# Banded attention of a two-layer decoder: two heads at a time, their scores alternating between the halves of the array's rows

## Chip, core and metric

The kernel runs on one core of a Trainium2 chip. The metric is the device time of one launch in microseconds. The core's engines work side by side, each through its own queue in order: TensorE (PE in the profile; its weight loads are shown apart as PEld), VectorE (DVE), ScalarE (ACT), GpSimd (POOL, hardly used here) and the DMA queue that SyncE (SP) issues.

## The reference

Two layers of a decoder trunk on 256 tokens with 2048 features. Each layer has a mixer (four mLSTM heads beside 16 heads of sliding-window attention) and an MLP of 8192 hidden features. The part that the change touches, cut down:

```python
# q (B,S,16,64); k, v (B,S,4,64): four query heads share one head of keys
# queries in blocks of T = 128; each block sees its own block of keys and the one before
scores = einsum('bnqhgd,bnkhd->bnhgqk', qb, kb)            # sums over 64 features
scores = where(valid, scores - slope_h * dist, -inf)       # 0 <= dist < 128
m = maximum(max(scores), sink_h)
p = exp(scores - m)
probs = p / (sum(p) + exp(sink_h - m))
out = einsum('bnhgqk,bnkhd->bnqhgd', probs, vb)
ha = rms_norm(out.reshape(B, S, 1024), g_attn_out)
```

The attention's result stands beside the mLSTM's, goes through the out-projection, a norm and the MLP.

## The kernel before

**Weights.** All weight matrices are streamed once from DRAM in loads of 1 MiB (tile `raw`, six buffers). Two k-tiles by 512 columns make a slab. ScalarE copies a slab to a rounded high part (`whi`, L232) and VectorE subtracts it for the low part (`wlo`, L236); four buffers of each. TensorE multiplies three products per k-tile (high by high, high by low, low by high), all at L329: 24 matmuls of 256 columns per slab where the weights are stationary (`qa`, `qm`, `km`, `up`), 12 of 512 columns where the tokens are (`vm`, `om`, `op`, `dn`). The loads of w_ada pass through the same `raw` buffers and are summed on VectorE (L204).

**Work beside the stream.** Everything else in a mixer is a set of Python generators (`Task`). Ahead of each slab's matmuls every task advances by one stage (`side`), so its instructions stand in the engines' queues between those of two slabs; after that a scheduler may shift them a little in the queues. PSUM tiles for this work come from a pool of four (`ps_x`, counted by `live["x"]`), tiles of 128x384 from a pool of seven (`live["w"]`).

**Attention** (`swa`, `swa_head`, `swa_out`). The query projection is laid out so that a tile `qa` of a unit u holds eight heads: heads 8u to 8u+3 on partitions 0 to 63, heads 8u+4 to 8u+7 on partitions 64 to 127; the keys `kaT` likewise. `swa` starts one head per slab, up to four in flight, in the order 0, 1, 2, ... 15. A head's stages are one slab apart:

1. Scores: two matmuls over 64 partitions into one PSUM tile `pss` (L591: 128 queries by 128 keys; L592: 128 queries by 256 keys). Each float32 matmul shows in the trace as two loads and two passes.
2. VectorE adds the distances times the slope (tile `s`, L595), takes the maxima (L598, L599) and the bias `nm` (L600).
3. ScalarE takes the exponentials and their sums (L602, L603).
4. Three transposes on TensorE into `pt` (L609).
5. ScalarE copies them to `sT` (L612).
6. Three matmuls with the values into `po` (L618 to L620), which collects four heads.

After four heads, `swa_out` normalises their 256 columns (L627 to L637) and sums squares (L84), and only then may the next group of four start. After the fourth group a norm over the 1024 features follows (L677 to L682), and the flag `swa` lets the mLSTM's outputs (`pn`, L852 to L854) begin. Their norms and gates (`rm`, `frs`, `va`) and the transposes `psct` (L909) lead to the out-projection `op`.

Of the kernel before, what the change touches and what calls it, by code (L numbers as in the profile page):

```python
# [27 lines left out]
# column offsets in the packed small parameters  # L28
# [5 lines left out]
# shape-only constants: identity | banded distances | causal bias  # L34
# [5 lines left out]
def hymba_kernel(ctx: ExitStack, tc: tile.TileContext, x_d, c_d, cols_d, cons_d, wada_d,  # L40
# [70 lines left out]
    # ("w", blocks of (unit, first k-tile), source) of weights; ("a", layer, vector, pair of feature tiles) of w_ada  # L111
# [9 lines left out]
    def weave(ws, *segments):  # L121
        """ws, with the entries ads of each segment (ads, start, upto) spread evenly over that range of ws."""
# [41 lines left out]
    # each entry in two loads  # L164
# [33 lines left out]
    def ada_op():  # L198
        """Sums over the input features for one tile of 128 output features."""
# [87 lines left out]
    class Unit:  # L287
        """Products with one block of 512 weight columns, accumulated in two PSUM banks."""
# [22 lines left out]
        def slabs_by_token(self, between):  # L311
            """Four slabs, all for the first token tile and then all for the second."""
# [42 lines left out]
    # gate rows (times the post-norm gain) broadcast over the partitions  # L355
# [17 lines left out]
    class PreNorm:  # L373
        """Residual update (with yg), RMSNorm, modulation and transposition of x."""
# [34 lines left out]
        def group(self, g, tok):  # L409
            """Transposed activations of four k-tiles, in two parts."""  # L410
# [18 lines left out]
        def turn_in(self, xnT, tok, g0=0):  # L429
            """Transposition of one token tile from k-tile 4 g0 on, before the modulation is known."""  # L430
# [12 lines left out]
        def modulate(self, e, xnT, hfp):  # L443
            """Two k-tiles of the activations."""
# [79 lines left out]
    for l in range(DEPTH):  # L524
# [59 lines left out]
        def swa_head(h, po):  # L584
            u, hh = h // 8, h % 8
            base, j = 64 * (hh // 4), hh % 4
            qt = fl["qa", u][base:base + 64, j, :]
            kt_ = kaT[base:base + 64, u, :]
            live["w"] += 1
            pss = xalloc(f"pss{L}_{h}")  # L590
            T.matmul(pss[:, 0:P], qt[:, TK[0]], kt_[:, TK[0]], start=True, stop=True)  # L591
            T.matmul(pss[:, P:3 * P], qt[:, TK[1]], kt_, start=True, stop=True)  # L592
            yield
            s = walloc(f"s{L}_{h}", 0)
            V.scalar_tensor_tensor(s, dist, -(2.0 ** (-8.0 * (h + 1) / 16.0)), pss[:, 0:384],  # L595
                                   ALU.mult, ALU.add)
            xdone()
            V.tensor_reduce(mx[:, h, 0:1], s[:, 0:P], AX.X, ALU.max)  # L598
            V.tensor_reduce(mx[:, h, 1:2], s[:, P:384], AX.X, ALU.max)  # L599
            V.tensor_scalar(nm[:, h, :], mx[:, h, :], sk[:, h:h + 1], -1.0, ALU.max, ALU.mult)  # L600
            yield
            A.activation(s[:, 0:P], s[:, 0:P], AF.Exp, bias=nm[:, h, 0:1], accum_out=sm[:, h, 0:1])  # L602
            A.activation(s[:, P:384], s[:, P:384], AF.Exp, bias=nm[:, h, 1:2], accum_out=sm[:, h, 1:2])  # L603
            yield
            while live["x"] > 3:
                yield
            pt = xalloc(f"pt{L}_{h}")
            for b in range(3):
                T.transpose(pt[:, b * P:(b + 1) * P], s[:, b * P:(b + 1) * P], ident)  # L609
            yield  # L610
            sT = walloc(f"sT{L}_{h}", 0)
            A.activation(sT, pt[:, 0:384], AF.Copy)  # L612
            xdone()
            yield
            vs = slice((h // 4) * 64, (h // 4) * 64 + 64)
            c0 = (h % 4) * 64
            o0, o1 = po[:, c0:c0 + 64], po[:, 256 + c0:256 + c0 + 64]
            T.matmul(o0, sT[:, 0:P], vat[:, 0, vs], start=True, stop=True)  # L618
            T.matmul(o1, sT[:, P:2 * P], vat[:, 0, vs], start=True, stop=False)
            T.matmul(o1, sT[:, 2 * P:3 * P], vat[:, 1, vs], start=False, stop=True)  # L620
            live["w"] -= 1

        def swa_out(g, po):
            """Normalisation of four heads and their sums of squares."""
            hs = slice(4 * g, 4 * g + 4)
            for b in range(2):
                V.tensor_tensor(es[:, hs, b], nm[:, hs, b], sk[:, hs], ALU.add)  # L627
            A.activation(es[:, hs, :], es[:, hs, :], AF.Exp)
            V.tensor_tensor(sm[:, hs, :], sm[:, hs, :], es[:, hs, :], ALU.add)
            V.reciprocal(sm[:, hs, :], sm[:, hs, :])  # L630
            yield
            o0 = (g % 2) * 256
            for b in range(2):
                if g % 2 == 0:
                    ha[g // 2, b] = ytile(f"ha{L}_{g // 2}_{b}")
                o = ha[g // 2, b][:, o0:o0 + 256]
                V.tensor_tensor(o.rearrange("p (h d) -> p h d", h=4),  # L637
                                po[:, b * 256:b * 256 + 256].rearrange("p (h d) -> p h d", h=4),
                                sm[:, hs, b:b + 1].broadcast_to([P, 4, 64]), ALU.mult)
            xdone()  # L640
            yield
            for b in range(2):
                square_sum(ha[g // 2, b][:, o0:o0 + 256], ssa[:, b, g:g + 1], f"jka{L}_{g}_{b}")
            yield

        def swa():
            while ("qa", 0) not in fl or "kv" not in fl:
                yield
            fly, nxt, outs, po = [], 0, [], None
            while nxt < 16 or fly or outs:  # L650
                for f in list(fly):
                    try:
# [3 lines left out]
                        live["q"] -= f[1] % 8 == 7  # L656
                        if f[1] % 4 == 3:
                            outs.append(swa_out(f[1] // 4, f[2]))
                            po = None
# [5 lines left out]
                ok = nxt < 16 and len(fly) < 4 and ("qa", nxt // 8) in fl  # L665
                if ok and nxt % 4 == 0:
                    ok = po is None and live["x"] <= 1
                    if ok:
                        po = xalloc(f"po{L}_{nxt // 4}")
                if ok and live["x"] <= 3 and live["w"] <= 6 and po is not None:  # L670
                    f = (swa_head(nxt, po), nxt, po)
# [48 lines left out]
        def gates():  # L720
# [29 lines left out]
            # log sigmoid(f) = min(f, 0) - log1p(exp(-|f|)), log1p(t) = log(w) + (t - (w - 1)) / w with w = 1 + t  # L750
# [16 lines left out]
            # u = i - b, g = running maximum of u (from the stabiliser before the chunk), m = b + g  # L767
# [10 lines left out]
            # columns: u (two chunks), u + B (first chunk), exp(-m) (two chunks)  # L778
# [25 lines left out]
        def mlstm_weights(h):  # L804
            """exp(u_s - g_t) times q k, [source position, target position]."""
# [215 lines left out]
        def evac_up_tokens(un, u):  # L1021
            """As evac_up, for products with tokens on the partitions."""
# [181 lines left out]
```

## Time and profile before

| | us |
|---|---|
| median of three timed runs | 2284.05 (2282.85 to 2285.39) |
| span of the profiled execution | 2283.6 |
| TensorE busy | 2195.6 |
| VectorE busy | 1690.7 |
| ScalarE busy | 1090.9 |
| start of layer 0's first score matmul | 160.8 |
| start of layer 1's first score matmul | 1256.0 |

The profile gives no time of its own for the profiled execution beside its span, from the first to the last instruction; the timed runs have no profile. In the views that follow, a row names line, engine, operation and tiles as out<-in, then counts and times. "64*128" on a matmul is the part of the array it uses, rows by columns. A merged timeline row "x2" covers two instructions from the first start to the last end. A matmul's shown length includes its way through the array; how fast a row of them goes is read from start to start.

### The profile page before, as it was taken

The page shows a single profiled execution, that of the slowest core. Times are in us where ns is not written, and L with a number is a line of the kernel's source. Part 1 is how long each engine was busy: PE and PEld are TensorE (multiplying, and loading weights), DVE is VectorE, ACT ScalarE, POOL GpSimd, SP SyncE. Part 2 cuts the span into 40 slices and gives each one's busy share as a digit, 9 for nine tenths or more (in the row PEclk, how much of TensorE's full clock was granted, in tenths as well). Part 3 has the DMA queues.
Part 4 walks back from the last instruction along what each step waited for, and adds up shares of the span by engine and source line. Part 5 has one row for each costly group of instructions (what it writes and reads, how often), then busy time and mean ns, then how long its engine had stood idle before and what let it go on. Part 6 is the DMA issues. An engine that isn't in the chain of part 4 may idle for free.

```text
span 2283.6 us, 33092 instructions
## 1 busy us (share of the span) xinstructions
PE 2195.6 (96%) x13322; PEld 1935.3 (85%) x13322; DVE 1690.7 (74%) x2282; ACT 1090.9 (48%) x1533; POOL 1.4 (0%) x14
## 2 busy tenths in 40 slices
PE   6789999899999999999989999989999999999998
PEld 5679777698898998989869988878898998998986
DVE  7988899787878877877577797957556656555556
ACT  4346663645444444434464566556443444444433
POOL 0000000000000000000000000000000000000000
PEclk9999999999999999999999999999999999999999
DMA  9997679497888888888538766845656666555551
GB/s 370 385 360 273 221 300 365 171 356 307 315 299 336 308 309 312 316 305 300 185 128 336 294 223 215 294 165 197 234 213 230 229 223 248 203 185 186 184 187 70
DMA packets 82363, 590.08 MB, mean 258 GB/s; under 512 B 9185, under 2 KB 9633, under 8 KB 10785
## 3 DMA queue, kind: packets, MB, share of 16 engines
q1 hardware_dynamic: 82210, 587.98, 69.4%
q8 instruction: 104, 1.70, 0.3%
q14 instruction: 49, 0.40, 0.0%
HBM read 585.81 MB, written 2.13 MB: 257 GB/s over the span
## 4 chain that ended last, share of the span: by engine, by line
PE 77%; DVE 4%; ACT 1%; issue 1%; DVEq 0%; ACTq 0%
PE up L329 32%; PE dn L329 31%; PE op L329 4%; PE qa L329 2%; PE vm L329 2%; PE om L329 1%; PE km L329 1%; PE qm L329 1%; PE kva L329 1%; DVE x L388 1%; DVE wlo L236 1%; PE pss L592 0%; PE pss L591 0%; ACT jkm L84 0%; PE psgate L730 0%
## 5 line engine op out<-in xcount | busy, mean ns | idle before, releaser
L236 DVE TENSOR_TENSOR wlo<-raw,whi 128x1024 fp32r<-128x1024 f32 x720 | 876.6, 1222 | 472.2 <-ACT whi L232 470.9
L232 ACT ACTIVATE whi<-raw 128x1024 fp32r<-128x1024 f32 x720 | 758.5, 1058 | 915.3 <-PE dn L329 376.0
L329 PE MATMUL up<-hthm,whi 128*128 128x256 f32 x1920 | 543.7, 283 | 0.0
L329 PE MATMUL up<-hthm,wlo 128*128 128x256 f32 x1920 | 543.3, 283 | 0.0
L329 PE MATMUL up<-htlm,whi 128*128 128x256 f32 x1920 | 543.2, 283 | 0.0
L204 DVE SCALAR_TENSOR_TENSOR raw<-raw,cact 128x2048 f32<-128x2048 f32 x192 | 437.3, 2285 | 4.1 <-DMA raw<-in_wada_dram 4.0
L329 PE MATMUL dn<-whi,sh 128*128 128x512 f32 x1024 | 404.1, 395 | 0.0
L329 PE MATMUL dn<-wlo,sh 128*128 128x512 f32 x1024 | 404.0, 395 | 0.0
L329 PE MATMUL dn<-whi,sl 128*128 128x512 f32 x1024 | 404.0, 395 | 0.0
L329 PEld LDWEIGHTS up<-htlm,whi 128*128 128x128 f32 x1920 | 368.4, 192 | 0.9
L329 PEld LDWEIGHTS up<-hthm,whi 128*128 128x128 f32 x1920 | 368.4, 192 | 0.9
L329 PEld LDWEIGHTS up<-hthm,wlo 128*128 128x128 f32 x1920 | 368.4, 192 | 0.0
L329 PEld LDWEIGHTS dn<-wlo,sh 128*128 128x128 f32 x1024 | 192.9, 188 | 45.0
L329 PEld LDWEIGHTS dn<-whi,sh 128*128 128x128 f32 x1024 | 193.0, 188 | 44.7 <-ACT sh L1034 0.4
L329 PEld LDWEIGHTS dn<-whi,sl 128*128 128x128 f32 x1024 | 192.9, 188 | 44.4 <-DVE sl L1035 0.2
L329 PE MATMUL op<-wlo,cth 128*128 128x512 f32 x256 | 99.6, 395 | 2.8 <-DVE wlo L236 2.8
L329 PE MATMUL op<-whi,cth 128*128 128x512 f32 x256 | 99.2, 396 | 2.6 <-ACT whi L232 2.6
L329 PE MATMUL op<-whi,ctl 128*128 128x512 f32 x256 | 100.2, 393 | 0.0
L329 PE MATMUL vm<-whi,htha 128*128 128x512 f32 x128 | 57.0, 447 | 28.7 <-ACT whi L232 18.7
L1064 DVE TENSOR_TENSOR ys<-ys,dn 128x512 f32<-128x512 f32 x112 | 75.4, 685 | 5.2 <-PE dn L329 4.6
L329 PE MATMUL qa<-htha,whi 128*128 128x256 f32 x256 | 73.2, 286 | 0.0
L329 PE MATMUL qa<-htla,whi 128*128 128x256 f32 x256 | 72.4, 283 | 0.0
(275 smaller groups left out, 2545.1 us busy)
## 6 DMA issues: line engine op xcount, KB each, us to landing
raw<-in_wada_dram SPq DMA_DIRECT2D x192, 1024.0 KB, 6.4
raw<-in_wdn_dram SPq DMA_DIRECT2D x128, 1024.0 KB, 5.0
raw<-in_wup_dram SPq DMA_DIRECT2D x120, 1024.0 KB, 4.9
raw<-in_win_dram SPq DMA_DIRECT2D x56, 1024.0 KB, 5.0
raw<-in_wout_dram SPq DMA_DIRECT2D x32, 1024.0 KB, 6.8
raw<-in_wst_dram SPq DMA_DIRECT2D x16, 1024.0 KB, 6.6
raw<-in_wsu_dram SPq DMA_DIRECT2D x8, 1024.0 KB, 6.2
gp<-gdr SPq DMA_DIRECT2D x4, 1024.0 KB, 4.7
```

What stands on the lines that cost most here:

```text
L204: V.scalar_tensor_tensor(w, w, 1.0, cact, ALU.mult, ALU.mult, accum_out=modc[l][:, v, j:j + 1])
L232: A.activation(hi, raw, AF.Copy)
L236: V.tensor_tensor(lo, raw, hi.bitcast(F32), ALU.subtract)
L329: T.matmul(o, a, w, start=not self.started[b], stop=last and i == 2, skip_group_check=True)
L388: V.scalar_tensor_tensor(xc, self.yg[c][tok], r, xc, ALU.mult, ALU.add)
L1064: V.tensor_tensor(yt, yt, ps[tok], ALU.add)
```

## The change

Two heads that share a `qa` tile's column but lie on its two halves (h and h + 4) form a pair. Their scores go into two PSUM tiles, and the four matmuls alternate: lower half, upper half, lower half, upper half. Vector and scalar stages run for both heads one after the other; transposes, copies and value matmuls for the first head of the pair, then, two slabs later, for the second. Pairs are started in the order (0,4), (1,5), (2,6), (3,7), (8,12), (9,13), (10,14), (11,15), one per slab, up to three in flight; a group that shares a `po` tile is now two pairs, for instance heads 0, 4, 1, 5. `swa_out` reads and writes its four heads with a stride. Nothing is computed differently. Comments are removed as well, which shifts the line numbers.

```diff
-        def swa_head(h, po):
-            u, hh = h // 8, h % 8
-            base, j = 64 * (hh // 4), hh % 4
-            qt = fl["qa", u][base:base + 64, j, :]
-            kt_ = kaT[base:base + 64, u, :]
-            live["w"] += 1
-            pss = xalloc(f"pss{L}_{h}")
-            T.matmul(pss[:, 0:P], qt[:, TK[0]], kt_[:, TK[0]], start=True, stop=True)
-            T.matmul(pss[:, P:3 * P], qt[:, TK[1]], kt_, start=True, stop=True)
-            yield
-            s = walloc(f"s{L}_{h}", 0)
-            V.scalar_tensor_tensor(s, dist, -(2.0 ** (-8.0 * (h + 1) / 16.0)), pss[:, 0:384],
-                                   ALU.mult, ALU.add)
...
+        def swa_pair(h, po):
+            u, j, heads = h // 8, h % 4, (h, h + 4)
+            live["w"] += 2
+            pss = [xalloc(f"pss{L}_{g}") for g in heads]
+            for c0, c1, tok, keys in ((0, P, 0, TK[0]), (P, 3 * P, 1, slice(0, S))):
+                for a in range(2):
+                    rows = slice(64 * a, 64 * a + 64)
+                    T.matmul(pss[a][:, c0:c1], fl["qa", u][rows, j, TK[tok]], kaT[rows, u, keys],
+                             start=True, stop=True)
+            yield
+            s = [walloc(f"s{L}_{g}", 0) for g in heads]
+            for a, g in enumerate(heads):
+                V.scalar_tensor_tensor(s[a], dist, -(2.0 ** (-8.0 * (g + 1) / 16.0)), pss[a][:, 0:384],
+                                       ALU.mult, ALU.add)
+                xdone()
+                V.tensor_reduce(mx[:, g, 0:1], s[a][:, 0:P], AX.X, ALU.max)
+                V.tensor_reduce(mx[:, g, 1:2], s[a][:, P:384], AX.X, ALU.max)
+                V.tensor_scalar(nm[:, g, :], mx[:, g, :], sk[:, g:g + 1], -1.0, ALU.max, ALU.mult)
+            yield
...
+            for a, g in enumerate(heads):
+                while live["x"] > 3:
+                    yield
+                pt = xalloc(f"pt{L}_{g}")
+                for b in range(3):
+                    T.transpose(pt[:, b * P:(b + 1) * P], s[a][:, b * P:(b + 1) * P], ident)
+                yield
+                sT = walloc(f"sT{L}_{g}", 0)
+                A.activation(sT, pt[:, 0:384], AF.Copy)
+                xdone()
+                yield
...
+            pairs = [8 * u + 2 * i + b for u in range(2) for i in range(2) for b in range(2)]
...
-                ok = nxt < 16 and len(fly) < 4 and ("qa", nxt // 8) in fl
-                if ok and nxt % 4 == 0:
+                ok = nxt < 8 and len(fly) < 3 and ("qa", nxt // 4) in fl
+                if ok and nxt % 2 == 0:
...
-                if ok and live["x"] <= 3 and live["w"] <= 6 and po is not None:
-                    f = (swa_head(nxt, po), nxt, po)
+                if ok and live["x"] <= 2 and live["w"] <= 5 and po is not None:
+                    f = (swa_pair(pairs[nxt], po), nxt, po)
```

What this does to the queues is shown at three places. First, TensorE's queue in layer 1 where the attention starts, between two slabs of `qa` (the number behind `pss_` is the head):

```order
 L329 MATMUL qa_1_11270<-htla_0_10420,whi_11211 128x256
 L329 MATMUL qa_1_11270<-htha_0_10419,wlo_11212 128x256
-L591 MATMUL pss_0_11309<-kaT_10809,qa_0_11277 128x128
-L592 MATMUL pss_0_11309<-kaT_10809,qa_0_11277 128x256
+L596 MATMUL pss_0_11309<-kaT_10809,qa_0_11277 128x128
+L596 MATMUL pss_4_11310<-kaT_10809,qa_0_11277 128x128
+L596 MATMUL pss_0_11309<-kaT_10809,qa_0_11277 128x256
+L596 MATMUL pss_4_11310<-kaT_10809,qa_0_11277 128x256
 L329 MATMUL qa_0_11269<-htha_0_10419,whi_11240 128x256
 L329 MATMUL qa_0_11269<-htla_0_10420,whi_11240 128x256
```

Heads 0 and 4 now stand between these two slabs, alternating; behind the next slab follow heads 1 and 5, and behind the six slabs after that no scores at all. The first transposes stand three slabs behind the scores, as before. All eight pairs of layer 1 look like this.

Second, TensorE's queue in layer 0, in the slabs of `om` (the scheduler's order; `pscol` are small transposes of the mLSTM's gates, 4 rows high, `pg` a matmul of theirs):

```order
L596 MATMUL pss_11_2424<-kaT_1291,qa_1_1315 128x128
L799 MATMUL pscol_2365<-cons,rows_2088 128x4 x2
L596 MATMUL pss_11_2424<-kaT_1291,qa_1_1315 128x256
L596 MATMUL pss_15_2425<-kaT_1291,qa_1_1315 128x128
L596 MATMUL pss_15_2425<-kaT_1291,qa_1_1315 128x256
L823 MATMUL pg_0_2430<-rows_2087,cons 128x256
```

Here heads 11 and 15 do not alternate, and two transposes stand between the matmuls of head 11. Heads 9 and 13 of layer 0 stand one after the other too, without anything between. The other six pairs of layer 0 alternate.

Third, VectorE's queue behind the first scores of layer 1, before:

```order
L595 SCALAR_TENSOR_TENSOR s_0_11347<-cons,pss_0_11309 128x384
L595 SCALAR_TENSOR_TENSOR s_1_11386<-cons,pss_1_11352 128x384
L598 TENSOR_REDUCE mx_10812<-s_0_11347 128x1
L599 TENSOR_REDUCE mx_10812<-s_0_11347 128x1
L236 TENSOR_TENSOR wlo_11380<-raw_11207,whi_11379 128x1024
L600 TENSOR_SCALAR nm_10813<-mx_10812,cols 128x2
```

and with the change:

```order
L601 SCALAR_TENSOR_TENSOR s_0_11350<-cons,pss_0_11309 128x384
L601 SCALAR_TENSOR_TENSOR s_4_11351<-cons,pss_4_11310 128x384
L604 TENSOR_REDUCE mx_10812<-s_0_11350 128x1
L605 TENSOR_REDUCE mx_10812<-s_0_11350 128x1
L604 TENSOR_REDUCE mx_10812<-s_4_11351 128x1
L606 TENSOR_SCALAR nm_10813<-mx_10812,cols 128x2
L605 TENSOR_REDUCE mx_10812<-s_4_11351 128x1
L236 TENSOR_TENSOR wlo_11391<-raw_11207,whi_11390 128x1024
L606 TENSOR_SCALAR nm_10813<-mx_10812,cols 128x2
```

The subtraction and a reduction of head 4 now stand ahead of head 0's bias `nm`; the work of two heads follows without a gap. Further on, at the end of layer 1's mixer, the first `pn` stands one slab later in TensorE's queue than before, behind slab 13 of the 16 slabs of `om` in place of slab 12, while the last `psct` of the concatenation stays ahead of the same slab of `op`.

More of the change, by code (lines that the diff above doesn't have):

```diff
@@ L582, in evac_qa, with by_group @@
             yield
[L584 to L600 removed]
+        def by_group(t, u, i):
+            return t.rearrange("p (u a i b) c -> p u i a b c", u=2, a=2, i=2, b=2)[:, u, i]
@@ L601, in swa_head @@
             yield
-            A.activation(s[:, 0:P], s[:, 0:P], AF.Exp, bias=nm[:, h, 0:1], accum_out=sm[:, h, 0:1])
-            A.activation(s[:, P:384], s[:, P:384], AF.Exp, bias=nm[:, h, 1:2], accum_out=sm[:, h, 1:2])
+            for a, g in enumerate(heads):
+                A.activation(s[a][:, 0:P], s[a][:, 0:P], AF.Exp, bias=nm[:, g, 0:1], accum_out=sm[:, g, 0:1])
+                A.activation(s[a][:, P:384], s[a][:, P:384], AF.Exp, bias=nm[:, g, 1:2],
+                             accum_out=sm[:, g, 1:2])
@@ L604, in swa_head @@
             yield
-            while live["x"] > 3:
-                yield
-            pt = xalloc(f"pt{L}_{h}")
-            for b in range(3):
-                T.transpose(pt[:, b * P:(b + 1) * P], s[:, b * P:(b + 1) * P], ident)
-            yield
-            sT = walloc(f"sT{L}_{h}", 0)
-            A.activation(sT, pt[:, 0:384], AF.Copy)
-            xdone()
-            yield
-            vs = slice((h // 4) * 64, (h // 4) * 64 + 64)
-            c0 = (h % 4) * 64
-            o0, o1 = po[:, c0:c0 + 64], po[:, 256 + c0:256 + c0 + 64]
@@ L618, in swa_head @@
[L618 to L625, printed above, removed]
-            for b in range(2):
[L627 to L639, printed above, removed]
+            for a, g in enumerate(heads):
+                while live["x"] > 3:
[3 more added lines that the diff above has]
+                    T.transpose(pt[:, b * P:(b + 1) * P], s[a][:, b * P:(b + 1) * P], ident)
+                yield
+                sT = walloc(f"sT{L}_{g}", 0)
+                A.activation(sT, pt[:, 0:384], AF.Copy)
+                xdone()
+                yield
+                vs = slice((g // 4) * 64, (g // 4) * 64 + 64)
+                c0 = (2 * a + h % 2) * 64
+                o0, o1 = po[:, c0:c0 + 64], po[:, 256 + c0:256 + c0 + 64]
+                T.matmul(o0, sT[:, 0:P], vat[:, 0, vs], start=True, stop=True)
+                T.matmul(o1, sT[:, P:2 * P], vat[:, 0, vs], start=True, stop=False)
+                T.matmul(o1, sT[:, 2 * P:3 * P], vat[:, 1, vs], start=False, stop=True)
+                live["w"] -= 1
@@ new lines, in swa_out @@
+        def swa_out(g, po):
+            u, i = g // 2, g % 2
+            nmg, smg, esg = [by_group(t, u, i) for t in (nm, sm, es)]
+            skg = sk.rearrange("p (u a i b) -> p u i a b", u=2, a=2, i=2, b=2)[:, u, i]
+            for b in range(2):
+                V.tensor_tensor(esg[:, :, :, b], nmg[:, :, :, b], skg, ALU.add)
+            A.activation(esg, esg, AF.Exp)
+            V.tensor_tensor(smg, smg, esg, ALU.add)
+            V.reciprocal(smg, smg)
+            yield
+            out = []
+            for b in range(2):
+                if i == 0:
+                    ha[u, b] = ytile(f"ha{L}_{u}_{b}")
+                o = ha[u, b].rearrange("p (a i d) -> p i a d", a=2, i=2)[:, i]
+                out.append(o)
+                V.tensor_tensor(o.rearrange("p a (h d) -> p a h d", h=2),
+                                po[:, b * 256:b * 256 + 256].rearrange("p (a h d) -> p a h d", a=2, h=2),
+                                smg[:, :, :, b].unsqueeze(3).broadcast_to([P, 2, 2, 64]), ALU.mult)
@@ L642, in swa_out @@
             for b in range(2):
-                square_sum(ha[g // 2, b][:, o0:o0 + 256], ssa[:, b, g:g + 1], f"jka{L}_{g}_{b}")
+                jk = jkp.tile([P, 512], BF16, tag="jk", name=f"jka{L}_{g}_{b}")
+                A.activation(jk[:, 0:256].rearrange("p (a d) -> p a d", a=2), out[b], AF.Square,
+                             accum_out=ssa[:, b, g:g + 1])
             yield
@@ L648, in swa @@
                 yield
+            pairs = [8 * u + 2 * i + b for u in range(2) for i in range(2) for b in range(2)]
             fly, nxt, outs, po = [], 0, [], None
-            while nxt < 16 or fly or outs:
+            while nxt < 8 or fly or outs:
                 for f in list(fly):
@@ L655, in swa @@
                         fly.remove(f)
-                        live["q"] -= f[1] % 8 == 7
-                        if f[1] % 4 == 3:
-                            outs.append(swa_out(f[1] // 4, f[2]))
+                        live["q"] -= f[1] % 4 == 3
+                        if f[1] % 2:
+                            outs.append(swa_out(f[1] // 2, f[2]))
                             po = None
```

2 lines of the change are left out of this document (1 added, 1 removed).

## The prediction

> **What bounds the kernel now.** I read the page first, for which engine the time belongs to.
>
> ```profile
> span 2283.6 us, 33092 instructions
> ...
> PE 2195.6 (96%) x13322; PEld 1935.3 (85%) x13322; DVE 1690.7 (74%) x2282; ACT 1090.9 (48%) x1533; POOL 1.4 (0%) x14
> ...
> PE 77%; DVE 4%; ACT 1%; issue 1%; DVEq 0%; ACTq 0%
> ```
>
> TensorE is busy 96% of the span and makes 77% of the chain that ended last, so a microsecond of TensorE work removed inside a TensorE-bound stretch is a microsecond off the end, as long as nothing else takes over there. Next I followed that chain through the stretch where layer 1's attention runs.
>
> ```profile
> 1256.07 0.41 PE pss L591 x2
> 1256.49 0.43 PE pss L592 x2
> 1256.92 3.06 PE qa L329 x24
> 1259.98 0.42 PE pss L591 x2
> 1260.40 0.43 PE pss L592 x2
> 1260.84 3.06 PE qa L329 x24
> ...
> 1275.43 0.22 PE po L619 x2
> ...
> 1276.21 2.87 PE qa L329 x24
> ```
>
> The chain never leaves TensorE here: each head's two score matmuls (two passes each) stand in line between the slabs of 24 weight matmuls. From one slab to the next with one head's scores between takes 1260.84 - 1256.92 = 3.92 us; a slab with no scores ahead of it takes 2.87. So one head's scores cost **1.04 us** (3.92 less 24 steps of 0.12), and the 32 heads of both layers 33 us, all of it on the path. The timeline shows what the 1.04 is made of:
>
> ```profile
> 1255.79 0.28 PE L329 MATMUL qa<-htha,wlo 128*128 128x256 f32 x1
> 1256.00 0.48 PE L591 MATMUL pss<-kaT,qa 64*128 64x128 f32 x2
> 1256.33 0.59 PE L592 MATMUL pss<-kaT,qa 64*128 64x256 f32 x2
> 1256.85 0.38 PE L329 MATMUL qa<-htha,whi 128*128 128x256 f32 x1
> 1257.07 0.28 PE L329 MATMUL qa<-htla,whi 128*128 128x256 f32 x1
> 1257.19 0.28 PE L329 MATMUL qa<-htha,wlo 128*128 128x256 f32 x1
> ```
>
> Weight matmuls start every 0.12 us (1257.07 to 1257.19), so the next start was due at 1255.91 and comes at 1256.00; the last one behind the scores, at 1257.07, marks 1256.95 as the time at which the rhythm is back. Between lie 1.04 us. The passes stream 0.11, 0.11, 0.22 and 0.22 us: 0.66 (128 and 256 columns, two passes each; the chain's 0.43 for L592 x2 is two of 0.22). The other **0.38** is paid for going from 128x128 to 64x128 and back: late first start, first load in the open, and the same again on the way out.
>
> **The change, part by part.** *Switches.* Thirty-two visits to the 64-row form become sixteen, with two heads each: 0.38 saved per pair if nothing else changes. The Trainium skill, "TensorEngine Tiling (Array Packing)", Tiling Modes, says that changing the tiling mode, not just the tile, drains the array; the 0.38 agrees, and by that rule A to B costs nothing. No row here shows a step from the lower half to the upper; should each of the three steps per pair cost half a switch (0.19), a pair would cost 3 x 0.19 - 0.38 = 0.19 more than now, 3 us over 16 pairs. That is the bad end of the unknown.
>
> *Overlap of the halves.* No row shows two halves at work together either, so I bound it. None: two heads stream 1.32 us and a pair takes 1.32 + 0.38 = 1.70 against 2.08, a gain of 0.38. Whole: they stream in the time of one, 0.66, a gain of 1.04. Between lies a bound from a row: L619 streams only 64 columns, yet its x2 takes 0.22, and the passes of 128 columns take the same 0.11. A load and its matmul thus do not go faster than 0.11 us, and a pair has eight of them, 0.88. In-order issue gives the same: A's second pass must follow A's first in the same half, so B's first runs beside A's second, and the line is eight steps of 0.11. I take **0.88**, the value that two readings of the rows give: a pair takes 1.26, a gain of **0.82**.
>
> *How many pairs.* In layer 1 all eight pairs stand A, B, A, B. In layer 0 six do. One (heads 9, 13) stands A, A, B, B, so only B's two short passes lie beside A's last: 1.10 + 0.38, a gain of 0.60. One (11, 15) is cut by two transposes of a 4-row tile: I give it 0.20. TensorE work falls by 8 x 0.82 = 6.6 in layer 1 and 6 x 0.82 + 0.8 = 5.7 in layer 0.
>
> *What the other engines let through.* The windows table (span of the window; busy PE, PEld, DVE, ACT, POOL; clock, DMA share, GB/s):
>
> ```profile
> 155.00:295.00 140.00, 140.00 (x905) 119.21 (x905) 122.60 (x215) 89.31 (x176) 0.00 (x0) 1.00 0.70 254
> 295.00:398.00 103.00, 98.70 (x442) 77.33 (x441) 100.14 (x212) 49.76 (x89) 0.00 (x0) 1.00 0.88 338
> 1256.00:1385.00 129.00, 129.00 (x921) 114.83 (x921) 108.14 (x196) 80.27 (x158) 0.00 (x0) 1.00 0.69 254
> ...
> 1420.00:1465.00 45.00, 44.65 (x210) 36.20 (x209) 42.22 (x125) 27.24 (x53) 0.00 (x0) 1.00 0.69 250
> ```
>
> Layer 1's attention (1256 to 1385) leaves VectorE 21 us idle and the DMA at 0.69: 6.6 us go through. Layer 0's (155 to 295) leaves VectorE 17.4 us, of which 5.7 would go, but from 295 to 398 VectorE is busy 100.14 of 103: what it has left behind by 295 it cannot catch up. Stretches that it enters earlier end earlier, so most of the gain passes; I take four fifths, 4.6 (bounds 0 and 5.7).
>
> *Charges.* Softmax work of a pair comes at once. The views of the tile s (minimum, median, maximum in ns) and the timeline around the first and the last of the 32 heads:
>
> ```profile
> L595 DVE SCALAR_TENSOR_TENSOR s<-cons,pss x32: 482/547/555, 163.0 to 1370.7; 128x384 f32<-128x384 f32 x32
> L598 DVE TENSOR_REDUCE mx<-s x32: 217/278/286, 165.7 to 1372.9; 128x1 f32<-128x128 f32 x32
> L599 DVE TENSOR_REDUCE mx<-s x32: 397/409/413, 165.9 to 1373.3; 128x1 f32<-128x256 f32 x32
> ...
> L602 ACT ACTIVATE s<-s,nm x32: 384/392/403, 171.0 to 1376.2; 128x128 f32<-128x128 f32 x32
> L602 ACT ACTIVATION_READ_ACCUMULATOR s<-s,nm x32: 185/187/193, 171.3 to 1376.5; 128x1 f32 x32
> L603 ACT ACTIVATE s<-s,nm x32: 491/494/502, 171.4 to 1376.6; 128x256 f32<-128x256 f32 x32
> ...
> 171.78 0.19 ACT L603 ACTIVATION_READ_ACCUMULATOR s<-s,nm 128x1 f32 x1
> ...
> 172.44 0.38 PE L609 MATMUL pt<-cons,s 128*128 128x128 f32 x2
> ...
> 1376.98 0.19 ACT L603 ACTIVATION_READ_ACCUMULATOR s<-s,nm 128x1 f32 x1
> ...
> 1377.76 0.28 PE L609 MATMUL pt<-cons,s 128*128 128x128 f32 x1
> ```
>
> The first head's exponentials end at 171.97 and its transposes start at 172.44, 0.47 later; the last head has 0.6. The new order puts the second head's subtraction (547) and its first reduction (278) ahead of the first head's maximum: 0.8 us later, in places with less than that to spare. But only the first head of a pair is hit; the second is transposed two slabs later. I charge 1.0 in all. At the end of layer 1's mixer:
>
> ```profile
> 1443.77 0.30 PE L909 MATMUL psct<-cons,va 128*128 128x128 f32 x1 [0.33 <-DVE va L884]
> ```
>
> TensorE already meets VectorE here (0.33 waited; VectorE busy 42.22 of 45). The first pn now stands one slab later in the queue while the last psct keeps its slab; VectorE has one product of w_ada and one low part less between. I charge 1.0 (bounds 0 and one slab, 2.7).
>
> *Sum.* 6.6 + 4.6 - 2.0 = 9.2 us off 2283.6: 2274.4. The timed median, 2284.05, lies 0.45 above the profiled span, so **2275**. With the charges at their bounds and four fifths between 0 and 1, 2272 to 2281.
>
> **The rivals.** *The halves take turns.* Then the change does not do what it says and only the switches go (none at the pair that is cut): 8 x 0.38 + 0.8 x 7 x 0.38 - 2.0 = 3.2, 2281. For it: no row shows overlap, and 0.38 alone is sure. Against it: operands and outputs of the halves lie on other partitions, and each head writes a PSUM tile of its own. Chance 0.28.
>
> *Whole overlap.* The second half rides free, a pair gains 1.04: 8 x 1.04 + 0.8 x (6 x 1.04 + 1.1) - 2.0 = 12.2, 2272. Against it: the 0.11 floor. The Trainium skill, "TensorE: Matmul & The Clock Gate", Part 3: Packing small matmuls, states this: matmuls on different row groups start some 4 ns apart, and a set lasts hardly longer than one. It also says that loads overlap running matmuls only when the row group differs; the trace disagrees, since 128-row loads run beside 128-row matmuls in every slab (PEld is busy 119 of 140 us while PE is busy 140). By the first rule the time would be 2272. Chance 0.10.
>
> *Layer 0 gives it back.* VectorE, full from 295 to 398, decides when that stretch ends: 6.6 - 2.0 = 4.6 is left, 2279.5. For it: 97% there; against it: its idle time before 295. Chance 0.10.
>
> *Softmax late, slower.* Each transposition moves behind a second head's work: 547 + 278 + 409 ns on VectorE and 392 + 494 + 2 x 187 on ScalarE, 2.5 us. Thirteen of the 32 heads have less to spare than that (0.47 at the first, 0.6 at the last), and their shortfalls, read head by head like these two, add up to 16 us; against a gain of 11.2 that is 4.8 slower, 2289. It decides once the waits add up to more than 11 us, 0.35 per head. Against it: the order keeps three slabs between scores and first transposes, and second heads get two more. Chance 0.12.
>
> **How the numbers follow.** Forecast 0.40 (2275), turns 0.28, whole overlap 0.10, layer 0 0.10, softmax 0.12. Faster by over 0.2% (4.6 us, about what a measurement can tell from no change) means below 2279.5: nearly all of the forecast, whole overlap, half of layer 0, a quarter of turns: 0.61. Slower: 0.11. Within: 0.28. The range reaches from 2269 (whole overlap with hardly a charge) to 2287 (part of the softmax case).
>
> **What would show it.** Slab to slab with a pair between: 2.88 + 1.26 = 4.14 us if I am right, 4.58 if the halves take turns, 3.92 if they overlap wholly, over 4.96 if half switches cost. Waits of pt on ACT should stay near 1 us; if they add up to many, the softmax rival holds. PE's idle time between 295 and 403 should not grow by more than 1 to 2 us, and psct on VectorE in layer 1 not beyond 1 to 3. I am wrong if the span falls by under 4 us with the pair at 4.14, for then the gain was taken back elsewhere.

## The result, and the profile after

| | before | after |
|---|---|---|
| median, us (lowest to highest, 4 runs each) | 2283.77 (2282.85 to 2285.39) | 2271.27 (2270.31 to 2273.51) |
| span of the profiled execution | 2283.6 | 2269.1 |
| time of the profiled execution | 2285.39 | 2270.89 |

The ratio is 0.9944, with a 95% interval of 0.9930 to 0.9958: 12.5 us faster, between 9.6 and 16.0. A profiled execution takes 1.8 us more than its span (2270.89 - 2269.1, and 2283.6 + 1.8 is 2285.4), so the profile of before shows the slowest of its four runs. The two profiles lie 14.5 us apart, the medians 12.5.

The page of the changed kernel, busy time by engine and the shares of the chain:

```profile
span 2269.1 us, 33077 instructions
...
PE 2182.2 (96%) x13322; PEld 1929.1 (85%) x13322; DVE 1689.8 (74%) x2282; ACT 1092.2 (48%) x1533; POOL 1.4 (0%) x14
...
PE 77%; DVE 4%; ACT 1%; issue 1%; DVEq 0%; ACTq 0%
```

The number of matmuls is the same, 13322; TensorE is busy 13.4 us less, and the bound is still TensorE. The chain through the start of layer 1's attention (start, length, engine, tile, line, instructions):

```profile
1248.09 0.86 PE pss L596 x8
1248.95 3.06 PE qa L329 x24
1252.01 0.86 PE pss L596 x8
1252.87 5.95 PE qa L329 x48
1258.82 0.33 PE pt L618 x3
```

From slab to slab with a *pair* between takes 1252.87 - 1248.95 = **3.92 us**, exactly what one *head* took before. Eight passes go by in the 0.86 in which four did (0.41 to 0.42 and 0.43 in the chain of before). The timeline merges the eight:

```profile
1247.81 0.28 PE L329 MATMUL qa<-htha,wlo 128*128 128x256 f32 x1
1248.02 0.93 PE L596 MATMUL pss<-kaT,qa 64*128 64x128 f32 x8
1248.88 0.38 PE L329 MATMUL qa<-htha,whi 128*128 128x256 f32 x1
1249.10 0.28 PE L329 MATMUL qa<-htla,whi 128*128 128x256 f32 x1
```

Its records show them singly. Start of each pass behind the first, in us (A: head 0, lower half; B: head 4, upper half; a record does not name the half, so it is told by the order of the queue and by the columns of each pass, 128 or 256):

```
A 0.000   B 0.006   A 0.213   B 0.220   A 0.325   B 0.331   A 0.543   B 0.550   next slab 0.855
```

The second head's passes start 6 to 7 ns behind the first head's and cost nothing more. The Trainium skill, "TensorE: Matmul & The Clock Gate", Part 3: Packing small matmuls, puts matmuls on different row groups some 4 ns apart; these rows agree but for 2 to 3 ns.

Where the time went, from the first starts of each stage's matmuls in the two traces (us):

| stretch | before | after | difference |
|---|---|---|---|
| layer 0: first scores to om | 97.38 | 91.51 | -5.87 |
| om to op | 62.28 | 61.09 | -1.19 |
| op to up | 112.93 | 112.12 | -0.81 |
| up to layer 1's first scores | 822.62 | 822.79 | +0.17 |
| layer 1: first scores to om | 125.45 | 117.97 | -7.48 |
| om to op | 57.18 | 55.72 | -1.46 |
| op to up | 100.29 | 102.42 | +2.13 |
| up to the end | 744.72 | 744.99 | +0.27 |

Sixteen pairs at 1.04 are 16.6 us, 8.3 per layer. Layer 0 kept 7.9 of its 8.3, layer 1 kept 6.8. In layer 1 one loss can be read off the timeline of this execution, at heads 9 and 13:

```profile
1309.71 0.55 DVE L601 SCALAR_TENSOR_TENSOR s<-cons,pss 128x384 f32<-128x384 f32 x1
1309.81 0.29 PEld L596 LDWEIGHTS pss<-kaT,qa 64*128 64x128 f32 x2
...
1310.31 0.52 PEld L596 LDWEIGHTS pss<-kaT,qa 64*128 64x128 f32 x6 [0.21 <-DVE s L601]
```

Head 13's scores need the PSUM tile that VectorE frees with a subtraction only at 1310.26 (1309.71 + 0.55); head 9 runs two passes alone, and the next slab starts 1.36 behind the first pass in place of 0.86: 0.5 lost. A second trace of the same kernel (e0_after, below) has no wait there, as its timeline shows in the first line; its list of waits has another, in the second line, where four slabs later a head's value matmuls wait for ScalarE's copy `sT`:

```profile
1309.75 0.93 PE L596 MATMUL pss<-kaT,qa 64*128 64x128 f32 x8
...
PEld po L627 <- ACT sT L621: 0.3, 1, 0.3
```

From first scores to om that trace takes 117.89, only 0.08 less than this one. So the loss at heads 9 and 13 is not a price of its own: without it a wait for ScalarE takes most of its place. From om to up another 0.67 is lost (2.13 - 1.46).

### The profile page after: what moved, and what is told of

Read it like the earlier page. It is cut to its first block, busy times and chain, and to the rows that moved or that the text cites. A ratio compares the mean times of both kernels' runs of the same rounds, so it can differ in the third digit from the quotient of the medians.

```text
span 2269.1 us, 33077 instructions
## 1 busy us (share of the span) xinstructions
PE 2182.2 (96%) x13322; PEld 1929.1 (85%) x13322; DVE 1689.8 (74%) x2282; ACT 1092.2 (48%) x1533; POOL 1.4 (0%) x14
## 3 DMA queue, kind: packets, MB, share of 16 engines
HBM read 585.81 MB, written 2.13 MB: 259 GB/s over the span
## 4 chain that ended last, share of the span: by engine, by line
PE 77%; DVE 4%; ACT 1%; issue 1%; DVEq 0%; ACTq 0%
PE up L329 32%; PE dn L329 31%; PE op L329 4%; PE qa L329 2%; PE vm L329 2%; PE om L329 2%; PE qm L329 1%; PE km L329 1%; PE kva L329 1%; DVE x L388 1%; DVE wlo L236 1%; PE pss L596 0%; ACT jkm L84 0%; PE psgate L746 0%; PE pt L618 0%
```

## The experiments

All times are medians. In brackets stands the ratio to the kernel before, timed beside it on the same chip, with its 95% interval. The changed kernel's number is e0_after's, 2271.6 (0.9943). The first four kernels and the last ran on that chip, the others on two more; the kernel before took 2284.9 on the first and 2284.7 and 2285.3 on the others, so a difference from 2271.6 across chips is uncertain by some 0.6 us beyond the scatter of the runs. Where a single trace is compared, it is from the first score matmul on.

**The changed kernel again.**

> The changed kernel once more, as the measure for the other kernels on the same chip. Every theory: 2271 us, 12 to 13 below the kernel before, and from slab to slab with a pair of scores between 3.92 us, so that a pair costs 1.04 us, what one head did (0.66 of streaming, 0.38 of switching to the 64-row form and back).

Measured: 2271.6 (ratio 0.9943, 0.9930 to 0.9955). As expected.

**Does the order of the queue matter?**

```diff
-            for c0, c1, tok, keys in ((0, P, 0, TK[0]), (P, 3 * P, 1, slice(0, S))):
-                for a in range(2):
+            for a in range(2):
+                for c0, c1, tok, keys in ((0, P, 0, TK[0]), (P, 3 * P, 1, slice(0, S))):
```

> Every pair's four score matmuls in the order A, A, B, B in place of A, B, A, B; nothing else. Theory 1, the halves of the array run on their own and it is enough that A and B stand next to each other: a pair still costs 1.04 us, 2271. Theory 2, what the prediction's number for heads 9 and 13 rested on, TensorE starts passes in the order of its queue, so that only B's two short passes lie beside A's last: a pair costs 1.10 + 0.38 = 1.48, 16 x 0.44 = 7 us more, 2278. Theory 3, TensorE looks ahead by a few passes only: between the two, with B's first pass starting behind A's first or second.

Measured: 2271.7 (0.9942, 0.9928 to 0.9955). The chain of this kernel at the same place, and the starts of the passes:

```profile
1248.71 0.86 PE pss L596 x8
1249.58 3.06 PE qa L329 x24
1252.64 0.86 PE pss L596 x8
```

```
queue: A A A A B B B B
A 0.000   B 0.013   A 0.213   B 0.227   A 0.325   B 0.338   A 0.543   B 0.557   next slab 0.862
```

B's first pass, fifth in the queue, starts 13 ns behind A's first and 0.2 us ahead of A's second. The third and fourth starts are passes of 128 columns, though the queue has A's two of 256 ahead of B's first. Passes of the two halves do not start in the order of the queue, so the alternation that the change writes out brings nothing; being neighbours does. Theory 2 falls. The Trainium skill, "PSUM — Partial Sum Buffer", Engine vs sequencer instructions, says that matmuls start and complete in program order; across the two halves this trace shows the opposite for the starts.

**Is it the halves, or merely the pairing?**

```diff
-            u, j, heads = h // 8, h % 4, (h, h + 4)
+            u, heads = h // 8, (h, h + 1)
...
-            pairs = [8 * u + 2 * i + b for u in range(2) for i in range(2) for b in range(2)]
+            pairs = [2 * p for p in range(8)]
```

> Pairs are made of two heads of the same half, (0,1), (2,3) and so on; their matmuls alternate and everything else is done two at a time as in the changed kernel. The switching is still paid once per two heads, but no half can run beside the other. Theory 1, overlap 0.66 and switching 0.38 are two separate gains per pair: a pair costs 2 x 0.66 + 0.38 = 1.70, 16 x 0.66 = 10.6 more than the changed kernel, 2281 to 2282, about 2 to 3 below the kernel before. Rival, the gain comes from handling two heads at a time (fewer visits, a denser stream of loads, another order on VectorE and ScalarE) and the halves have no part in it: 2271 to 2273. Rival, pairing costs 2 us or more in waits elsewhere, as the prediction charged: 2284 or more.

Measured: 2281.9 (0.9986, 0.9978 to 0.9995), 10.3 above the changed kernel where 10.6 was due. The chain:

```profile
1255.97 3.07 PE qa L329 x24
1259.04 1.50 PE pss L597 x8
1260.55 5.96 PE qa L329 x48
```

Slab to slab 4.58 (1260.55 - 1255.97), so a pair costs 1.70: the same eight passes one after the other, and one switch in place of two. Overlap of the halves carries 0.66 of the 1.04, as Theory 1 has it. (The heads also come in another order here, and with the normalisation of the kernel before; the next experiment shows that these are worth nothing.) The kernel is also the prediction's rival "the halves take turns", built on purpose: 2281.

**Is it the new order of heads?** One head per slab, in the new order and with the strided normalisation; the cut is against the kernel before.

```diff
+            order = [8 * u + 4 * a + 2 * i + b for u in range(2) for i in range(2) for b in range(2) for a in range(2)]
...
-                    f = (swa_head(nxt, po), nxt, po)
+                    f = (swa_head(order[nxt], po), nxt, po)
```

> One head per slab as in the kernel before, but in the changed kernel's order of heads (0, 4, 1, 5, ...) and with its strided normalisation of four heads. No pair. Theory 1: the order and the strides are worth nothing, 2283 to 2285, a head still costs 1.04 and neighbouring heads, a slab of 24 weight matmuls apart, gain nothing from lying on different halves. Rival, part of the 12.5 us comes from the order or the strided normalisation: 2280 or less.

Measured: 2285.28 against 2284.94 of before (1.0000, 0.9991 to 1.0008). Order and strides are worth nothing.

**Is the 0.38 a switch of the array's form?**

```diff
-                    rows = slice(64 * a, 64 * a + 64)
-                    T.matmul(pss[a][:, c0:c1], fl["qa", u][rows, j, TK[tok]], kaT[rows, u, keys],
+                    T.matmul(pss[a][:, c0:c1], fl["qa", u][:, j, TK[tok]], kaT[:, u, keys],
```

> The pair's four score matmuls run over all 128 rows, both halves at once, so that the array's form stays 128 by 128; both heads get the sum of the two heads' products, which is not what the scores should be. Nothing can overlap, but nothing is switched. Theory 1, the 0.38 is the price of going to the 64-row form and back: a pair costs 8 passes, 1.32, which is 0.28 more than the changed kernel's pair; 16 x 0.28 = 4.5 more, 2276. Rival, the 0.38 belongs to any visit to other tiles between two slabs (float32 operands, another tile of PSUM): 1.70 per pair, 2282 as with both heads on the same half.

This kernel leaves out the separation of the two heads' scores; it serves the timing alone. Measured: 2275.41 (0.9960, 0.9945 to 0.9975), 3.8 above the changed kernel where 4.5 was due. The chain:

```profile
1249.65 1.31 PE pss L595 x8
1250.96 2.87 PE qa L329 x24
1253.83 1.31 PE pss L595 x8
```

Eight passes take 1.31, and the slab behind them is back at 2.87 from 3.06: no price for going in or out. Together with the two kernels before, a pair has three prices that add up: 1.31 (no switch, no overlap), 1.70 (switch, no overlap), 1.04 (switch and overlap).

**Do streams still count when they overlap?** Every score matmul twice, halves alternating.

```diff
-            for c0, c1, tok, keys in ((0, P, 0, TK[0]), (P, 3 * P, 1, slice(0, S))):
+            for c0, c1, tok, keys in ((0, P, 0, TK[0]), (P, 3 * P, 1, slice(0, S))) * 2:
```

> Every score matmul of the changed kernel is issued twice, the halves alternating as before (A, B, A, B, A, B, A, B); the second time overwrites the same values. Theory 1, a pair costs 0.38 of switching and the streams of one half, 0.66 each time: a pair costs 1.70, 16 x 0.66 = 10.6 more than the changed kernel, 2282. Rival, what a pair costs is mostly a fixed 1.04 for the visit, and streams are nearly free behind it: below 2276. Rival, the prediction's floor of 0.11 for each load and its matmul over both halves (16 more of them, 0.88): 16 x 0.88 = 14, 2285. Halves that take turns: 16 x 1.32 = 21, 2293.

Measured: 2274.49 (0.9955, 0.9942 to 0.9969), 2.9 above the changed kernel. By the total the rival "a fixed 1.04 for the visit" would hold; the chain says otherwise:

```profile
1248.10 3.07 PE qa L330 x24
1251.17 1.51 PE pss L597 x16
1252.68 5.96 PE qa L330 x48
```

A pair takes 1.51 in place of 0.86, 0.65 more, Theory 1's price to 0.01, at each of the sixteen. The visits are thus 10.5 us longer in all, and 7.6 of it came back at another place. This expectation missed in its total and held in its mechanism.

**How far ahead does TensorE look?** The doubled matmuls in blocks, and then three times in blocks.

```diff
+            for a in range(2):
+                for c0, c1, tok, keys in ((0, P, 0, TK[0]), (P, 3 * P, 1, slice(0, S))) * 2:
```

> The same doubled score matmuls, in two blocks: A, A, A, A, then B, B, B, B. This asks how far down its queue TensorE reaches for work of the other half. Theory 1, each half has a line of its own and B starts at once whatever stands ahead of it: a pair costs 1.70 as with the alternating order, 2282. Theory 3, TensorE looks only a few passes ahead: with a reach of the four passes that heads A, A, B, B need, B starts when half of A's eight passes are issued, and a pair costs 0.38 + 0.66 + 1.32 = 2.36 or less, up to 16 x 0.66 = 10.6 more, 2282 to 2293, and B's first start in the trace tells the reach.

> Every score matmul three times, in blocks: head A's twelve passes, then head B's twelve. With two blocks of eight passes B's first pass started 6 ns behind A's fifth, with three more of A's ahead of it. Theory 3, TensorE reaches over a fixed number of waiting passes: B's first starts with A's ninth, about 1.42 us behind A's first (0.10 more than eight passes of 0.165 on average), and the visit lasts some 0.66 longer than with two blocks. Rival, the point is a share of the block (half): B's first starts with A's seventh, at 1.09. Rival, B waits for the whole first round of A's values (a tile of PSUM written a second time) and starts where it did, at 0.76.

Measured: 2287.49 (1.0010, 1.0001 to 1.0019) and, in two runs, 2307.7 (1.0098, 1.0080 to 1.0117). First starts in one visit of each kernel (the first pass on a half that stood idle lasts 373 ns in the records, one behind another pass of its half 269 to 272, which tells B1 from A's passes):

```
two blocks of 8:    A1 0.000  A2 0.213  A3 0.325  A4 0.543  A5 0.759  B1 0.765  A6 0.868  ...  next slab 2.269
three, blocks of 12: A1 0.000  ...  A8 1.198  A9 1.414  B1 1.420  A10 1.523  ...  next slab 3.579
```

B starts 5 to 6 ns behind A's pass number n - 3 in both: fifth of eight, ninth of twelve, and in the kernel with A, A, B, B the first of four. So B may have **three** passes of the other half still waiting ahead of it, no more. In the orders tried here the halves overlap wholly as long as a head brings no more than four passes; these heads have exactly four. Theory 1's "whatever stands ahead of it" falls, Theory 3 holds with this number. The Trainium skill, "TensorE: Matmul & The Clock Gate", Part 1, Architectural detail, gives TensorE a queue 64 deep with a partial reorder window; what these runs show of it across the halves is four passes.

**What does each layer bring?** Pairs in layer 1 alone.

```diff
+            if l == 1:
...
+                        f = (swa_pair(pairs[nxt], po), nxt, po)
...
+            else:
...
+                        f = (swa_head(order[nxt], po), nxt, po)
```

> Pairs in layer 1 only; layer 0 takes one head at a time in the order 0, 4, 1, 5, ... of the earlier experiment, which was worth nothing by itself. Theory 1, a pair's gain in layer 0 passes through whole, though VectorE is full there from 295 to 398 us: layer 1 alone brings 8 x 1.04 = 8.3 less about 1.5 that is lost behind it, 6.8; 2278, 6.8 above the changed kernel's 2271.6 less layer 1's share, so layer 0's pairs bring 6 to 8. Rival, the prediction's: layer 0 gives back a fifth or more of what it saves, and layer 1 brings more than 8: 2276 or less.

Measured: 2278.8 (0.9972, 0.9964 to 0.9981), 5.9 below the kernel before where 6.8 was due; the changed kernel's ratio is 0.0029 lower, 6.6 us, and that is layer 0's part, uncertain by some 3 us either way. So layer 0 gives about as much as layer 1. Whether it lets through four fifths of its 8.3, as the prediction had it, or nearly all cannot be told from these times: 6.6 is four fifths, and the traces in the table above say 7.9. In this kernel's own trace layer 1 gains 6.85 as forecast (7.56 and 1.46 less 2.17), while layer 0's stretch from op to up takes 115.15, 2.8 more than in the kernel with single heads in the same order.

**Where did the doubled kernel's 7.6 us go?** Scores doubled in layer 0 only.

```diff
-            for c0, c1, tok, keys in ((0, P, 0, TK[0]), (P, 3 * P, 1, slice(0, S))):
+            for c0, c1, tok, keys in ((0, P, 0, TK[0]), (P, 3 * P, 1, slice(0, S))) * (2 - l):
```

> Score matmuls issued twice, alternating, in layer 0 only; layer 1 as in the changed kernel. Doubling in both layers took 2.9 us where 16 x 0.66 = 10.6 were due, although each pair was 0.66 longer in the trace. Theory 4, the missing time is layer 0's: with the longer matmuls the scheduler puts the end of layer 0's mixer in another order (gate rows a slab earlier, fewer products of w_ada behind the start of the out-projection), and the out-projection takes 108.9 us in place of 112.5; 8 x 0.66 - 3.5 leaves at most 1.8, and 2269 to 2273.5 for the whole, though layer 0's TensorE work is 5.2 longer. Rival, the missing time is in layer 1: 2276 to 2277.

Measured: 2271.91 (0.9940, 0.9927 to 0.9952), the changed kernel's time within 0.3, with 5.2 us more for TensorE in layer 0. The waits of TensorE in layer 0's out-projection (what waited, for whom: us in total, times, longest), in the changed kernel:

```profile
PE op L329 <- DVE wlo L236: 2.9, 4, 1.6
...
PE op L329 <- ACT whi L232: 1.8, 1, 1.8
PE psct L925 <- DVE ha L698: 0.9, 1, 0.9
PE op L329 <- DVE ctl L930: 0.7, 1, 0.7
```

and with layer 0's scores doubled:

```profile
PE op L329 <- DVE wlo L236: 2.5, 4, 1.4
...
PE psct L925 <- ACT va L882: 0.4, 1, 0.4
PE psct L925 <- DVE rm_v L97: 0.3, 1, 0.3
```

Waits of 6.3 us became 3.2. The windows from the first op to the first up, changed kernel and doubled (length, then busy PE, PEld, DVE, ACT, POOL with instructions, clock, DMA share, GB/s):

```profile
312.89:425.35 112.46, 99.79 (x438) 77.98 (x436) 98.63 (x209) 56.07 (x104) 0.00 (x0) 0.98 0.75 287
```

```profile
318.11:427.10 108.99, 98.68 (x435) 78.31 (x435) 97.58 (x204) 55.49 (x104) 0.00 (x0) 0.98 0.73 280
```

With longer score matmuls the compile-time scheduler moves work beside the stream: VectorE has 204 instructions in this stretch in place of 209. That the order does it, and not merely the time that VectorE gains, is what the pairs on the same half speak for. Their visits are as long (1.50 against 1.51), VectorE's instructions from 45 us ahead of op to 60 behind it come in the changed kernel's order, and the stretch takes 114.18; its clock was 0.95, and without the 2.4 us that TensorE was busy longer there (102.21 against 99.79) it would be some 111.8. Every kernel with doubled or tripled scores in layer 0 takes 108.9 to 109.0 there, every kernel that keeps the changed kernel's or the earlier order 112.0 to 115.2. Which of the moved instructions decides it was not tried. In the kernel with both layers doubled this gives 3.5 of the 7.6. Between layer 0's first scores and op another 1.3 comes back, in layer 1 0.4 up to om (no value matmul waits there) and 0.6 from om to op. The start of that execution, 1.8 us earlier, would fill the rest, but it is a matter of the single execution and not of the kernel, so about 1.8 of the 7.6 stays open.

**Can the switch be shared further?** Four heads in one visit.

```diff
-                if ok and live["x"] <= 2 and live["w"] <= 5 and po is not None:
-                    f = (swa_pair(pairs[nxt], po), nxt, po)
-                    next(f[0])
-                    fly.append(f)
-                    nxt += 1
+                if nxt < 8 and len(fly) < 1 and ("qa", nxt // 4) in fl and live["x"] == 0 and live["w"] <= 3:
+                    po = []
+                    live["w"] += 4
+                    for n in (nxt, nxt + 1):
+                        f = (swa_pair(pairs[n], po), n, po)
+                        next(f[0])
+                        fly.append(f)
+                    nxt += 2
```

> Two pairs (four heads) issue their scores in one visit, A, B, A, B, C, D, C, D; the softmax of the second pair starts one slab behind the first's, and the output tile po is taken when the first values are multiplied. Theory 1: a visit costs 0.38 + 2 x 0.66 = 1.70 where two pairs cost 2.08, so 8 x 0.38 = 3.0 are saved on TensorE, 2268 to 2269 if nothing else moves. Against it: all four tiles of PSUM for such work must be free before a visit, so the last heads' values stand three slabs later in layer 1, and the mLSTM's outputs behind them. Rival, that tail takes the 3 us back: 2271 to 2275. Rival, VectorE and PSUM hold up the scores (four subtractions of 0.55 before the tiles are free): 2275 or more.

Measured: **2266.32** (0.9917, 0.9903 to 0.9930), 5.3 below the changed kernel, the fastest of all (5.9 by the ratios, since this is another chip). Four heads take 1.51 in six of the eight visits; layer 0's first waits for its queries and takes 2.43, and its last is split by other work:

```profile
1246.56 1.51 PE pss L595 x16
1248.07 8.84 PE qa L329 x72
```

The tail did cost what was feared (om to up in layer 1: 160.27 against 158.13), but first scores to om fell by 4.5. Part of that is a shift: 6 of the 48 transposes and 18 of the 90 value matmuls that stood ahead of the first om now stand behind it. From first scores to up layer 1 takes 2.3 less. From first score to end the two traces differ by 3.3, of which 3.0 was forecast; layer 0's out-projection, at 108.31, is among the short ones, though om to op ahead of it is 4.2 longer. The rest of the 5.3 is not settled by single traces.

**The softmax as late as it can be made.**

```diff
-            if h % 2:
-                yield
             s = [walloc(f"s{L}_{g}", 0) for g in heads]
```

> Four heads in one visit as before, but the softmax of the second pair no longer waits one slab: VectorE takes all four heads at once (four times 0.55 + 0.28 + 0.41 and the bias, over 5 us, where a slab of weight matmuls lasts 2.9). Two groups of four heads then follow each other eight slabs apart, as in the changed kernel, not nine. This is the prediction's rival softmax late, made as strong as the kernel allows. Theory: four buffers of low parts cover a burst of VectorE of 5 us, and the transposes come late by little; about 1 us gained at the end of layer 1's mixer, 2264 to 2267 (the four heads a slab apart: 2266.3). Rival: transposes wait for the exponentials and slabs for their low parts, 2 us or more per group, eight groups: 2270 and more.

Measured: 2268.42 (0.9929, 0.9916 to 0.9943), between the expected 2264 to 2267 and the rival's 2270, and 2.1 above the version with a slab between, whose interval it overlaps. From first score to end the traces agree (2105.49 and 2105.34); this execution's first score came 1.6 later. Layer 0's out-projection takes 113.9 here, 5.6 more than there, but om to op ahead of it is 6.2 shorter. So waiting a slab or not makes no difference that these runs show, and the 1 us expected from it does not appear. The view of the tile pt, and which engine sat idle around it:

```profile
L617 PE MATMUL pt<-cons,s x96: 270/273/283, 172.3 to 1358.4; 128*128 128x128 f32 x96
L620 ACT ACTIVATE sT<-pt x32: 462/482/493, 173.4 to 1358.7; 128x384 f32<-128x384 f32 x32
its engine sat idle before it (us, times) until:
  PE pt L617: 3.1, 7
```

The only idle time is ScalarE's, waiting for the transposes; TensorE's transposes never wait for the exponentials, even with four heads in a burst. The prediction's rival "softmax late" does not happen here.

## Why the prediction was right, and where it was off

The forecast was 2275 (2269 to 2287), faster with 0.61; measured 2271.27. Direction and range held, and so did the mechanism in kind: one switch for two heads, and overlap of the halves. That the overlap is whole was not the forecast but a rival with a chance of 0.10, and its 2272 is the nearer number. That it is so near is partly luck: its sum takes off 12.2, while the traces show 14.5. Term by term:

- **Switches, 0.38 per pair, A to B at no cost: right.** 1.70 on one half against 2.08 for two heads; 1.31 without any switch. No half-switch between the halves shows.
- **Overlap of the halves, 0.44 of the 0.82: too small; this is the term that was mis-sized.** It measured 0.66, so a pair gains 1.04. Both readings that gave the middle value failed. The 0.11 per load and matmul holds within one half (two passes of 128 columns there start 0.11 apart at the least), not across both (B's starts lie 6 to 7 ns behind A's); and B's first pass need not wait for A's second. The pair at 3.92 is the lowest of the four marks named, whole overlap. One argument against taking turns was wrong as it stands: only the operands of the halves lie on other partitions, while both score tiles are 128x384 and take all 128; what keeps the outputs apart is the tile of its own.
- **Layer 0's two odd pairs, 0.60 and 0.20: wrong for the same reason.** Heads 9 and 13, queued A, A, B, B, overlap wholly (next start 0.863 behind the first). Heads 11 and 15 lose only the two passes ahead of the transposes: six passes follow in 0.86.

```profile
259.85 0.49 PE L596 MATMUL pss<-kaT,qa 64*128 64x128 f32 x2
260.26 0.28 PE L799 MATMUL pscol<-cons,rows 4*128 4x4 f32 x2
260.47 0.93 PE L596 MATMUL pss<-kaT,qa 64*128 64x256 f32 x6
261.33 0.69 PE L823 MATMUL pg<-rows,cons 4*128 4x256 f32 x2
```

- **Layer 0, 4.6 let through: too little.** 7.9 of 8.3 arrived in the trace, 6.6 by the kernel with layer 1 alone, so the share may be four fifths or nearly all; the saving of 5.7 that it was taken of was itself too small. TensorE reached the out-projection 7.1 us sooner, and its waits for VectorE and ScalarE there hardly grew (6.1 before, 6.5 after). As far as the runs show, the length of that stretch goes with the order of VectorE's queue (108 to 109 us, or 112 and more), not with how early TensorE comes.
- **Softmax charge 1.0: about its size, at other places.** No transposition waited for an exponential, as the charge had it. What waited were value matmuls, for ScalarE's copy of the transposes (in layer 0, where 0.3 of the load's 0.6 holds up the matmuls, in both traces of the kernel), and in layer 1 head 13 for a PSUM tile (0.5) in one trace or value matmuls again (0.3) in the other:

```profile
PEld po L627 <- ACT sT L621: 0.6, 1, 0.6
```

- **Tail of layer 1, 1.0: 0.67.**
- **Profiled span against median, 0.45: wrong.** The profiled execution of before was 1.6 above the median, so the traces show 14.5 where the medians show 12.5. That error went the other way and hid 2 us of the first; that the two partly cancel is luck.

In sum: 9.2 forecast, 14.5 in the traces (7.9 + 6.8, less 0.4 in the stretches behind the mixers, and 0.3 from the time before the first scores), 12.5 in the medians.

## What to carry to other kernels

Matmuls over 64 rows that lie on the two halves of the array stream in the time of one half when they are neighbours in the queue (eight passes in the 0.86 of four), alternating or in blocks of up to four passes; look for such neighbours before writing out an alternation. Price a visit to another array form as streams plus one switch, and put as much as fits into one visit: four heads for one switch beat two. A total can hide a term: the doubled scores cost 10.5 us in the trace and 2.9 in the time, in part because a compile-time scheduler put other work elsewhere, so read the term itself from start to start. And a wait in one trace is not yet a price: look whether a second trace of the same kernel has it.

## What the hardware showed that was not expected

- Passes on the two halves need not start in the queue's order; their starts lie 6 to 7 ns apart when they alternate and 13 to 14 when they are queued A, A, B, B. The reach is three waiting passes (B starts with A's 5th of 8, 9th of 12); each pass has a load of its own, so these runs do not tell whether passes or instructions are counted.
- The two passes of each float32 matmul overlap with those of the other half pass by pass: eight in 0.86, sixteen in 1.51.
- Going from the 128-row form to the 64-row form and back costs 0.38 us in all (1.70 less 1.31 for the same eight passes); no cost of going from one half to the other shows (1.04 is 0.66 and that 0.38).
- Single executions reach their first score matmul between 158.1 and 161.6 us, while the 644 us from layer 0's dn to layer 1's vm repeat within 0.2. Traces of one execution are best compared from a common matmul on.
